# Hybrid DiT layer on one core: norm columns turned by TensorE before they are stored, and another order of the seven products and of their weight sums

## The chip, the cores and the metric

The kernel runs on one core of a Trainium2 chip. The metric is device time in microseconds (us) of one execution; the time before is the median of three executions. A separate execution was recorded by the hardware profiler, and all rows below are of that one. PE is TensorE (its weight loads, PEld, overlap it), DVE is VectorE, ACT is ScalarE, POOL is GpSimd and SP is SyncE; POOL and SP here do little but issue transfers.

## The reference, cut to what matters

One layer for 512 tokens of width 1024: a token mixer (retention, 2-D Fourier mixing, spatial gating) between two modulated norms, then an MLP with squared ReLU between two more. All data are float32.

```python
mod = silu(c) @ w_mod + b_mod
sh1, sc1, gt1, sh2, sc2, gt2 = split(mod, 6)
h = modulate(rms_norm(x, g_pre_mix), sh1, sc1)
y = token_mixer(h, ...)          # sum over branches: sigmoid gate * (branch @ w), then @ w_out
x = x + gt1 * rms_norm(y, g_post_mix)
h2 = modulate(rms_norm(x, g_pre_mlp), sh2, sc2)
x = x + gt2 * rms_norm(relu(h2 @ w_up) ** 2 @ w_down, g_post_mlp)   # hidden width 4096
```

## The kernel before

**Precision.** A float32 product is made of three matmuls: every operand is split into a high part (written by ACT: `whi`, `rhi`, `phi`) and a low part (raw minus high part, by DVE: `wlo`, `rlo`, `plo`), and high x high, high x low and low x high are summed in PSUM (L132 to L134, L1025, L1152). Weights arrive as 512 KB chunks, 128 x 1024, on SP's queue.

**Stages in time.** Modulation and norms; the projections with retention, Fourier and gating; the gates (to about 340 us), the branch products ("abc" loop, eight turns of `m`), the output projection `out_proj` (to about 440 us); then the MLP in four quarters of the hidden width. For quarters q = 0, 1, 2 the down product is `down(q)`; then `up(q + 1, m)` makes the next quarter's hidden units in eight turns of 24 matmuls. The last quarter's down product is plain (`last_down`).

**The seven products.** `down(q)` is one level of Strassen's scheme: seven products (`seventh`, L1141) of 24 matmuls each. Their weights are quarters of `w_down` or sums of these: L11, S1 = L21 + L22, L12, S3 = L11 + L21, S2 = S1 + L11, L22, S4 = S2 + L12, each in two halves a = 0, 1. Their other operands are hidden units: `r1`, `r2` (R11, R21, R22) or sums of them: `t13` (T1, T3), `t24` (T2, T4), made on DVE with `sums_13` and `sums_24` and split by ACT and DVE. The products stand in three pairs of PSUM banks, `chain`, `side` and `own`; after most products `collect` (L1155) adds the pair into `y2`, on DVE except in quarter 0, where those that set `y2` go to ACT. A later product that continues the same pair has to wait for the `collect` that reads it.

**Weight sums.** `weights_to(q, upto)` makes weights in the order of the table `order` (L1029). `rawL` gets L11 (SP) and then, by a DVE add (L1059), L21, so it holds S3. `rawS` is loaded with L21 (L1057) and grows by accumulating transfers: L22 at L1060 (S1), L11 at L1069 (S2), L12 at L1072 (S4). Accumulating transfers are issued by POOL, each after the split of the sum before.

**What sets the order.** PE, SP and POOL keep the order of the program text, whose calls put weights some products ahead. ACT and DVE are ordered by a list scheduler at build time, in which splits and collects have a raised priority. All engines work in order: what stands behind a waiting instruction waits too.

**Modulation rows.** `background()` loads one 512 KB chunk of `w_mod` (POOL, L388) and does one product of it with c as a DVE instruction of 1.28 us (L241), giving a column of 128 values of `mod`. The calls are spread over the gates, the abc loop, and, for the last group (gt2), over the up loop of quarter 1.

**The norm columns.** `gg1` = gt1 * g_post_mix and `gg2` = gt2 * g_post_mlp come out as 128 x 8 columns (value p + 128 k at partition p, column k). `spread_row` (L848) turns such a column into a row that is the same on all partitions: L851 writes it into DRAM in row order, 1024 pieces of 4 bytes, and L853 loads that back to 128 partitions. `gg1r` is used by `out_proj` (z, L907), `gg2r` by `last_down`. Both transfers are on POOL's queue. `ident`, the unit matrix used for transposes on PE (L929), is loaded by SP.

Of the kernel before, what the change touches and what calls it, by code (L numbers as in the profile page):

```python
# [35 lines left out]
def kernel(ctx: ExitStack, tc: tile.TileContext, i: dict, out: bass.AP):  # L36
# [764 lines left out]
    for n in range(12, 24):  # L801
        gate(n)
        background()

    gg1 = const.tile([P, KT], F32, name="gg1")
    gs2 = const.tile([P, KT], F32, name="gs2")
# [7 lines left out]
    merged = []  # L814
    for m in range(KT):
        w = chunk("abc", m)
        pss = [bank() for _ in range(3)]
        for k in (4, 5, 6, 7, 0, 1, 2, 3):
            b = 0 if k < 4 else (1 if k < 6 else 2)
            sl = slice(128 * k, 128 * k + 128)  # L820
            mm3(pss[b], (w[0][:, sl], w[1][:, sl]), hl(branch_in[k]), k in (0, 4, 6), k in (3, 5, 7))
        acc = []
        for b in (1, 2, 0):
            n = 8 * b + m
            t = tmp(f"mg{b}")
# [21 lines left out]

    def spread_row(col, name):  # L848

        d = dram.tile([D], F32, name=name + "_d")  # L850
        nc.gpsimd.dma_start(out=d.rearrange("(k p) -> p k", p=P), in_=col)  # L851
        r = slot([P, D], F32, name)
        nc.gpsimd.dma_start(out=r, in_=d.unsqueeze(0).broadcast_to([P, D]))  # L853
        return r
# [3 lines left out]
    for t in range(TT):  # L858
        nc.sync.dma_start(out=xts[t], in_=i["x"][t])
    pad = slot([P, D], F32, "pad")  # L860
    ident, used = pad[:, 0:P], [P]
    nc.sync.dma_start(out=ident, in_=i["eye"])
    gg1_row = spread_row(gg1, "gg1r")
    h2 = [slot([P, 2, L], F32R, "h2") for _ in range(KT)]
# [105 lines left out]
    def sums_13(a0, a1, b1):  # L970
# [6 lines left out]
        return ta[:, E0]  # L977

    def sums_24(t1, b1, b0):

# [47 lines left out]

    order = [(x, a) for x in ("L11", "S1", "L12", "S3", "S2", "L22", "S4") for a in range(2)]  # L1029
    ws_ = {}  # L1030
# [3 lines left out]
    def weights_to(q, upto):  # L1034

        while made.setdefault(q, 0) < min(upto, len(order)):
            x, a = order[made[q]]
# [15 lines left out]
            if x == "L11":  # L1053
                rawL[a] = slot([P, D], F32, "rawL")
                nc.sync.dma_start(out=rawL[a], in_=l11)
                rawS[a] = slot([P, D], F32, "rawS") if q else raw_pool.tile([P, D], F32, name="rawS", tag="wmod2", bufs=2)
                nc.gpsimd.dma_start(out=rawS[a], in_=l21)  # L1057
                parts(pair(), rawL[a])
                V.tensor_tensor(out=rawL[a], in0=rawL[a], in1=rawS[a], op=ALU.add)  # L1059
                nc.gpsimd.dma_start(out=rawS[a], in_=l22, accum_op=ALU.add)  # L1060
            elif x in ("L12", "L22"):
# [3 lines left out]
            elif x == "S3":  # L1065
                parts(pair(), rawL[a])
            elif x == "S1":
                parts(pair(slot), rawS[a], 0)
                nc.gpsimd.dma_start(out=rawS[a], in_=l11, accum_op=ALU.add)  # L1069
            elif x == "S2":  # L1070
                parts(pair(), rawS[a])
                nc.gpsimd.dma_start(out=rawS[a], in_=l12, accum_op=ALU.add)  # L1072
            else:
                parts(pair(), rawS[a])

    early, tas = [], []

    def up_first_done(half):
# [14 lines left out]
        if half:  # L1093
            weights_to(0, 8)
            for k in range(4):
                sums_24(tas[k], late[1][:, k], early[1][:, k])
            for k in range(4):
                split(r2[k][:, 0, E1], r2[k][:, 1, E1], late[1][:, k])

# [37 lines left out]
    def down(q, following):  # L1137
# [3 lines left out]
        def seventh(pss, w, x, first, ahead):  # L1141
            for a in range(2):
                weights_to(q, ahead + a)
                if ahead + a > len(order):
                    following(ahead + a - len(order))
                wa = ws_.pop((w, a))
# [18 lines left out]
        collect(chain, 0, 0, False, True)  # L1165
        seventh(own, "L12", "R21", True, 7)
        collect(own, 0, 0, False)
        seventh(side, "S3", "T3", True, 9)
        collect(side, 1, 1, True, True)
        seventh(chain, "S2", "T2", False, 11)  # L1170
        collect(chain, 0, 1, True, True)
        seventh(side, "L22", "T4", False, 13)
        collect(side, 0, 1, True)
        seventh(chain, "S1", "T1", False, 15)
        collect(chain, 1, 1, True)
        seventh(chain, "S4", "R22", False, 16)
# [6 lines left out]
    for q in range(3):  # L1183
# [3 lines left out]
        for n, m in enumerate(turns if q < 2 else range(KT)):  # L1187
            up(q + 1, m, 7 - n if q < 2 else 2)
            if q == 0:
                background()  # L1190
            if q < 2 and n >= 4:
                weights_to(q + 1, n - 3)
        if q == 0:
            V.tensor_tensor(out=gg2, in0=mod[:, 5], in1=vecs[:, G_POST2], op=ALU.mult)
    gg2_row = spread_row(gg2, "gg2r")
    xts[:] = [slot([P, D], F32, "xt") for _ in range(TT)]
# [133 lines left out]
```

## Time and profile before

| what | us |
|---|---|
| median of three executions | 785.85 (784.85, 787.02, 785.85) |
| the profiled execution: its own time | 782.69 |
| its span, first to last instruction | 780.2 |
| PE busy | 761.8 (98%) |
| DVE busy | 547.4 (70%) |
| ACT busy | 398.0 (51%) |
| POOL busy | 61.0 (8%) |

The span is what the rows can account for; around it lie 2.5 us of start and end. The profiled execution was 3.2 us below the median of the three. In the rows a time in front is counted from the start of the span, the next figure is the duration, and square brackets hold the idle time of that engine before the instruction and what ended it. "a<-b" names what is written and read.

### The profile page before, as it was taken

How to read it: one execution, taken by the hardware profiler on the slowest of the kernel's cores; microseconds unless marked ns; L12 is line 12 of the kernel's file. 1: busy time of each engine (PE TensorE's matmuls, PEld its weight loads, DVE VectorE, ACT ScalarE, POOL GpSimd, SP SyncE). 2: the span in 40 equal slices, each digit the busy share in tenths (PEclk: the TensorE clock that was granted, in tenths of full speed). 3: DMA queues.
4: the chain of work that ended last, by engine and by line, in shares of the span. 5: the costliest groups of instructions: out<-in, count | busy, mean ns of one | idle time of the engine just before them, and what ended most of it. 6: DMA issues, size and time to landing. Idle time of an engine off the chain costs nothing.

```text
span 780.2 us, 9628 instructions
## 1 busy us (share of the span) xinstructions
PE 761.8 (98%) x3628; PEld 636.3 (82%) x3628; DVE 547.4 (70%) x853; ACT 398.0 (51%) x599; POOL 61.0 (8%) x107
## 2 busy tenths in 40 slices
PE   9999999999999999999999999899997999999996
PEld 6888888888888878888888998688876887888885
DVE  6999997777889546589748648637974468634544
ACT  6337557658887534233246457436632466236411
POOL 1061000000000101101000000001210001100000
PEclk9999999999999999999999999999999999999999
DMA  9954242643333458667423634447855526834211
GB/s 349 383 186 136 95 134 67 206 152 104 113 108 100 143 181 276 218 194 269 145 98 109 217 55 108 108 155 242 196 99 176 173 61 168 260 117 136 81 55 54
DMA packets 34461, 121.44 MB, mean 156 GB/s; under 512 B 4184, under 2 KB 4448, under 8 KB 34416
## 3 DMA queue, kind: packets, MB, share of 16 engines
q1 hardware_dynamic: 24768, 86.17, 32.3%
q0 software_dynamic: 9632, 34.66, 16.7%
q8 instruction: 28, 0.46, 0.3%
q14 instruction: 17, 0.14, 0.1%
q10 hardware_dynamic: 16, 0.01, 0.0%
HBM read 116.62 MB, written 4.20 MB: 155 GB/s over the span
## 4 chain that ended last, share of the span: by engine, by line
PE 66%; issue 19%; DVE 7%; DMA 5%; ACT 2%; POOL 1%; DVEq 0%; POOLq 0%; ACTq 0%
PE ps L134 15%; PE ps L133 15%; PE ps L132 14%; PE pu L1025 6%; PE kq L357 5%; PE chain L1152 4%; DMA rawS<-in_w_down 4%; PE side L1152 2%; DMA wmod<-in_w_modT 2%; DVE wlo L128 1%; PE warm L190 1%; DVE y L1162 1%; POOL wmod L388 1%; DVE t L128 1%; DVE wlo L109 1%
## 5 line engine op out<-in xcount | busy, mean ns | idle before, releaser
L134 PE MATMUL ps<-h,wlo 128*128 128x512 f32 x448 | 174.8, 390 | 1.9 <-DVE wlo L109 1.9
L132 PE MATMUL ps<-h,whi 128*128 128x512 f32 x448 | 175.1, 391 | 0.0
L133 PE MATMUL ps<-h,whi 128*128 128x512 f32 x448 | 174.6, 390 | 0.0
L106 ACT ACTIVATE whi<-raw 128x1024 fp32r<-128x1024 f32 (+1 forms) x97 | 100.8, 1041 | 138.0 <-PE ps L133 86.5
L109 DVE TENSOR_TENSOR wlo<-raw,whi 128x1024 fp32r<-128x1024 f32 (+1 forms) x97 | 116.4, 1200 | 71.9 <-ACT whi L106 71.7
L134 PEld LDWEIGHTS ps<-h,wlo 128*128 128x128 f32 x448 | 84.1, 188 | 20.2 <-DVE wlo L109 2.7
L132 PEld LDWEIGHTS ps<-h,whi 128*128 128x128 f32 x448 | 84.1, 188 | 17.7 <-ACT whi L106 0.4
L133 PEld LDWEIGHTS ps<-h,whi 128*128 128x128 f32 x448 | 84.2, 188 | 17.3
L241 DVE CUSTOM_DVE_ANT_0 wmod<-wmod,cb,vecs 128x1024 f32<-128x1024 f32 x32 | 41.0, 1281 | 28.2 <-DMA wmod<-in_w_modT 28.2
L388 POOL DMA_DIRECT2D wmod<-in_w_modT x32 | 17.1, 535 | 328.8 <-PE ps L134 253.8
L1025 PE MATMUL pu<-h,rhi 128*128 128x256 f32 x224 | 39.9, 284 | 0.2 <-DVE pad L881 0.2
L1152 PE MATMUL chain<-whi,r 128*128 128x512 f32 x96 | 31.9, 404 | 4.0 <-DVE y L1162 4.0
L1025 PEld LDWEIGHTS pu<-h,rhi 128*128 128x128 f32 x224 | 34.4, 192 | 0.5 <-DVE pad L881 0.4
L1152 PE MATMUL side<-whi,t 128*128 128x512 f32 x96 | 30.6, 390 | 0.0
L1025 PE MATMUL pu<-h,rlo 128*128 128x256 f32 x112 | 29.8, 283 | 0.0
L106 ACT ACTIVATE rhi<-raw 128x1024 fp32r<-128x1024 f32 x17 | 17.8, 1056 | 22.6 <-DMA raw<-in_w_out 16.3
L128 DVE TENSOR_TENSOR wlo<-rawS,whi 128x1024 fp32r<-128x1024 f32 x12 | 14.6, 1225 | 18.0 <-ACT whi L127 18.0
L357 PE MATMUL kq<-h,whi 128*128 128x512 f32 x112 | 27.0, 392 | 0.0
L127 ACT ACTIVATE whi<-rawS 128x1024 fp32r<-128x1024 f32 x12 | 12.7, 1060 | 27.9 <-DMA rawS<-in_w_down 18.7
L1152 PEld LDWEIGHTS chain<-whi,r 128*128 128x128 f32 x96 | 18.7, 195 | 8.4 <-issue 4.4
L357 PEld LDWEIGHTS kq<-h,whi 128*128 128x128 f32 x112 | 21.0, 188 | 4.8 <-ACT h L253 0.4
L109 DVE TENSOR_TENSOR rlo<-raw,rhi 128x1024 fp32r<-128x1024 f32 x17 | 20.6, 1222 | 5.5 <-ACT rhi L106 5.5
(359 smaller groups left out, 1641.3 us busy)
## 6 DMA issues: line engine op xcount, KB each, us to landing
wmod<-in_w_modT POOLq DMA_DIRECT2D x32, 512.0 KB, 3.6
raw<-in_w_up SPq DMA_DIRECT2D x32, 512.0 KB, 3.5
raw<-in_w_gate SPq DMA_DIRECT2D x24, 512.0 KB, 3.9
rawS<-in_w_down POOLq DMA_DIRECT2D x24, 512.0 KB, 5.4
raw<-in_w_down SPq DMA_DIRECT2D x20, 512.0 KB, 4.6
wmod<-in_w_modT SPq DMA_DIRECT2D x16, 512.0 KB, 8.6
raw<-in_w_kq SPq DMA_DIRECT2D x8, 512.0 KB, 7.1
raw<-in_w_v SPq DMA_DIRECT2D x8, 512.0 KB, 4.2
```

The costliest lines, as they stand in the source:

```text
L106: S.activation(out=hi, in_=raw, func=AF.Copy)
L109: rest = lambda: V.tensor_tensor(out=lo, in0=raw, in1=f32(hi), op=ALU.subtract)
L127: S.activation(out=dst_hi, in_=src, func=AF.Copy)
L128: V.tensor_tensor(out=dst_lo, in0=src, in1=f32(dst_hi), op=ALU.subtract)
L132: PE.matmul(ps, w[0], x[0], start=first, stop=False)
L133: PE.matmul(ps, w[0], x[1], start=False, stop=False)
L134: latest[0] = PE.matmul(ps, w[1], x[0], start=False, stop=last)
L241: return V.tensor_tensor_reduce(out=prod, in0=wt, in1=cvec, scale=1.0, scalar=bias_col, op0=ALU.mult, op1=ALU.add, accum_out=dst_col)
L357: PE.matmul(kq[n], w[sub % 2][:, 128 * n:128 * n + 128], hs[k][:, sub // 2], start=k == 0 and sub == 0, stop=False)
L388: load = nc.gpsimd.dma_start(out=t, in_=i["w_modT"][j, k])
L1025: latest[0] = PE.matmul(ps, w[a][:, 128 * m:128 * m + 128], x[b], start=k == 0 and (a, b) == parts[0] and m % 2 == 0, stop=k == KT - 1 and ...
L1152: latest[0] = PE.matmul(pss[p], st[b], mv[c], start=first and a == 0 and kk == 0 and n == 0, stop=a == 1 and kk == 1 and n == 2, skip_grou ...
```

## The change

1. **Norm columns.** `to_dram` turns the column by a PE transpose into an 8 x 128 tile of PSUM, ACT copies it into `pad`, and one transfer of eight 512-byte pieces writes it to DRAM. For `gg1` this stands in the abc loop at m = 2, for `gg2` in the last up loop at n = 5. The unit matrix is loaded earlier, by POOL instead of SP.
2. **Weight sums.** L21 gets into `rawL` by an accumulating transfer (L1086 of the changed kernel) instead of the DVE add. The load of `rawS` with L21 and the accumulation of L22 stand back to back on POOL, at S1's place.
3. **Quarter 0.** `sums_24` is cut in two: the first halves before the products (`sums_2`), the second halves (`second_24`), which only the sixth product's operand T4 needs, after S3's collect; the splits of R22 come after S2's collect.
4. **Quarters 1 and 2.** The weights are made in the order S1, L11, S3, S2, L12, L22, S4, begun at the first turn of the up loop instead of the fifth; the products run L11, S3, S2, L12, S1, L22, S4.
5. **The last modulation rows** are loaded and multiplied in the up loop of the last quarter, two a turn, instead of that of quarter 1.

```diff
+    def to_dram(col, name):
+        ps = bank("psv")
+        PE.transpose(ps[0:KT, 0:P], col, ident)
+        row = pad[0:KT, (4 if name == "gg1" else 5) * P:][:, 0:P]
+        S.copy(out=row, in_=ps[0:KT, 0:P])
+        d = dram.tile([KT, P], F32, name=name + "_d")
+        nc.gpsimd.dma_start(out=d, in_=row)
+        return d
...
     for m in range(KT):
+        if m == 2:
+            gg1_d = to_dram(gg1, "gg1")
...
-        d = dram.tile([D], F32, name=name + "_d")
-        nc.gpsimd.dma_start(out=d.rearrange("(k p) -> p k", p=P), in_=col)
         r = slot([P, D], F32, name)
-        nc.gpsimd.dma_start(out=r, in_=d.unsqueeze(0).broadcast_to([P, D]))
+        nc.gpsimd.dma_start(out=r, in_=d.rearrange("k p -> (k p)").unsqueeze(0).broadcast_to([P, D]))
...
+    def sums_2(t1, b1):
+        tb = tmp("tb")
+        V.scalar_tensor_tensor(out=tb[:, E0], in0=t1, scalar=-1.0, in1=b1, op0=ALU.mult, op1=ALU.subtract)
+        t24.append(aux([P, 2, L], F32R, "t24"))
+        split(t24[-1][:, 0, E0], t24[-1][:, 1, E0], tb[:, E0])
+        tbs.append(tb)
+    def second_24(k):
+        tb = tbs[k]
+        V.scalar_tensor_tensor(out=tb[:, E1], in0=tb[:, E0], scalar=-1.0, in1=early[1][:, k], op0=ALU.mult, op1=ALU.subtract)
+        split(t24[k][:, 0, E1], t24[k][:, 1, E1], tb[:, E1])
...
             if x == "L11":
                 rawL[a] = slot([P, D], F32, "rawL")
                 nc.sync.dma_start(out=rawL[a], in_=l11)
-                rawS[a] = slot([P, D], F32, "rawS") if q else raw_pool.tile([P, D], F32, name="rawS", tag="wmod2", bufs=2)
-                nc.gpsimd.dma_start(out=rawS[a], in_=l21)
                 parts(pair(), rawL[a])
-                V.tensor_tensor(out=rawL[a], in0=rawL[a], in1=rawS[a], op=ALU.add)
-                nc.gpsimd.dma_start(out=rawS[a], in_=l22, accum_op=ALU.add)
+                nc.gpsimd.dma_start(out=rawL[a], in_=l21, accum_op=ALU.add)
...
             elif x == "S1":
-                parts(pair(slot), rawS[a], 0)
+                rawS[a] = slot([P, D], F32, "rawS") if q else raw_pool.tile([P, D], F32, name="rawS", tag="wmod2", bufs=2)
+                nc.gpsimd.dma_start(out=rawS[a], in_=l21)
+                nc.gpsimd.dma_start(out=rawS[a], in_=l22, accum_op=ALU.add)
+                parts(pair(slot), rawS[a])
                 nc.gpsimd.dma_start(out=rawS[a], in_=l11, accum_op=ALU.add)
...
+        else:
+            seventh(side, "S3", "T3", True, 7)
+            collect(side, 1, 1, True, True)
+            seventh(chain, "S2", "T2", False, 9)
+            collect(chain, 0, 1, True, True)
+            seventh(own, "L12", "R21", True, 11)
+            collect(own, 0, 0, False)
+            seventh(chain, "S1", "T1", False, 13)
+            collect(chain, 1, 1, True)
+            seventh(side, "L22", "T4", False, 15)
+            collect(side, 0, 1, True)
         seventh(chain, "S4", "R22", False, 16)
         collect(chain, 1, 0, False, True)
...
-            if q == 0:
-                background()
-            if q < 2 and n >= 4:
-                weights_to(q + 1, n - 3)
-        if q == 0:
-            V.tensor_tensor(out=gg2, in0=mod[:, 5], in1=vecs[:, G_POST2], op=ALU.mult)
-    gg2_row = spread_row(gg2, "gg2r")
+            if q < 2:
+                weights_to(q + 1, (1, 2, 2, 2, 3, 4, 4, 4)[n])
+            if q == 2 and n < 4:
+                background(2)
+            if q == 2 and n == 5:
+                V.tensor_tensor(out=gg2, in0=mod[:, 5], in1=vecs[:, G_POST2], op=ALU.mult)
+                gg2_d = to_dram(gg2, "gg2")
+    gg2_row = spread_row(gg2_d, "gg2r")
```

DVE in quarter 0, from the low part of S3's second half to that of S2 (`wlo<-rawS`), before the change. `t_..<-tb` are low parts of `t24`, `r_..<-late` those of R22.

```order
L128 TENSOR_TENSOR wlo<-rawL,whi 128x1024
L1162 TENSOR_TENSOR y_4336<-y_4336,own 128x512
L128 TENSOR_TENSOR t_4292<-ta,t_4292 128x512
L128 TENSOR_TENSOR t_4306<-tb,t_4306 128x512
L983 SCALAR_TENSOR_TENSOR tb<-tb,early 128x256
L982 SCALAR_TENSOR_TENSOR tb<-ta,late 128x256 x2
L983 SCALAR_TENSOR_TENSOR tb<-tb,early 128x256 x2
...
L128 TENSOR_TENSOR t_4324<-tb,t_4324 128x512
L128 TENSOR_TENSOR r_3980<-late,r_3980 128x256
L128 TENSOR_TENSOR wlo<-rawS,whi 128x1024 x2
```

The same place of the changed kernel.

```order
L128 TENSOR_TENSOR wlo<-rawL,whi 128x1024
L1190 TENSOR_TENSOR y_4327<-y_4327,own 128x512
L128 TENSOR_TENSOR t_4295<-ta,t_4295 128x512
L128 TENSOR_TENSOR t_4308<-tb,t_4308 128x256
L128 TENSOR_TENSOR t_4313<-tb,t_4313 128x256
L995 SCALAR_TENSOR_TENSOR tb<-ta,late 128x256
L128 TENSOR_TENSOR wlo<-rawS,whi 128x1024
L128 TENSOR_TENSOR t_4318<-tb,t_4318 128x256
L995 SCALAR_TENSOR_TENSOR tb<-ta,late 128x256
L128 TENSOR_TENSOR wlo<-rawS,whi 128x1024
```

The first low part of S2 has moved ahead of most sums and splits of `t24` and ahead of all those of R22 that stood in front of it.

DVE in quarter 1 before, from the collect of S3 (`side`) to that of S4 (the last `chain`); `wlo<-raw` at L128 is the low part of L22, and the `wlo<-rawS` rows are those of S4.

```order
L1162 TENSOR_TENSOR y_4338<-y_4338,side 128x512
L128 TENSOR_TENSOR wlo<-raw,whi 128x1024 x2
L1162 TENSOR_TENSOR y_4335<-y_4335,chain 128x512
L1162 TENSOR_TENSOR y_4336<-y_4336,chain 128x512
L128 TENSOR_TENSOR wlo<-rawS,whi 128x1024 x2
L1162 TENSOR_TENSOR y_4335<-y_4335,side 128x512
L1162 TENSOR_TENSOR y_4336<-y_4336,side 128x512
L109 TENSOR_TENSOR wlo<-raw,whi 128x1024
L1162 TENSOR_TENSOR y_4337<-y_4337,chain 128x512
L1162 TENSOR_TENSOR y_4338<-y_4338,chain 128x512
```

The changed kernel from the collect of L12 (`own`) on.

```order
L1190 TENSOR_TENSOR y_4327<-y_4327,own 128x512
L128 TENSOR_TENSOR wlo<-rawS,whi 128x1024
L1190 TENSOR_TENSOR y_4328<-y_4328,chain 128x512
L1190 TENSOR_TENSOR y_4329<-y_4329,chain 128x512
L128 TENSOR_TENSOR wlo<-rawS,whi 128x1024
L1190 TENSOR_TENSOR y_4326<-y_4326,side 128x512
L1190 TENSOR_TENSOR y_4327<-y_4327,side 128x512
L109 TENSOR_TENSOR wlo<-raw,whi 128x1024 x2
L1190 TENSOR_TENSOR y_4328<-y_4328,chain 128x512
L1190 TENSOR_TENSOR y_4329<-y_4329,chain 128x512
```

S1's collect (the first pair of `y_4328` and `y_4329`) now stands ahead of the second low part of S4, and L22's product lies between S1's and S4's.

POOL's transfers around the end of the abc loop, before.

```order
L388 DMA wmod2_3113<-in_w_modT 128x1024
L1057 DMA rawS_4093<-in_w_down 128x1024
L1057 DMA rawS_4127<-in_w_down 128x1024
L853 DMA gg1r_3305<-gg1r_d_3303 128x1024
L922 DMA kept0_3402<-xt_3293 128x1024
```

The changed kernel there.

```order
L816 DMA gg1_d_3027<-pad_2923 8x128
L388 DMA wmod2_3073<-in_w_modT 128x1024
L388 DMA wmod2_3120<-in_w_modT 128x1024
L1095 DMA rawS_4156<-in_w_down 128x1024
L1096 DMA rawS_4156<-in_w_down 128x1024
L1095 DMA rawS_4188<-in_w_down 128x1024
L1096 DMA rawS_4188<-in_w_down 128x1024
L867 DMA gg1r_3308<-gg1_d_3027 128x1024
L933 DMA kept0_3405<-xt_3300 128x1024
```

The load of `gg1r` now has two accumulating transfers (L1096) in front of it, each of which waits until the load of the same `rawS` has landed.

## Rows read from the trace of the kernel before

**Rows 1.** The page, busy time of the engines in the whole span.

```profile
PE 761.8 (98%) x3628; PEld 636.3 (82%) x3628; DVE 547.4 (70%) x853; ACT 398.0 (51%) x599; POOL 61.0 (8%) x107
```

**Rows 2.** Waits of PE: engine, line, waited for; us in total, times, longest.

```profile
PE chain L1152 <- DVE y L1162: 4.0, 1, 4.0
PE chain L1152 <- DVE wlo L128: 2.6, 1, 2.6
PE ps L134 <- DVE wlo L109: 1.9, 2, 1.5
...
PE side L1152 <- DVE wlo L128: 1.1, 1, 1.1
PE own L1152 <- DVE wlo L128: 0.5, 1, 0.5
```

**Rows 3.** Stretches: length, then busy us of PE, PEld, DVE, ACT, POOL, clock, DMA.

```profile
493.00:498.00 5.00, 5.00 (x22) 4.16 (x23) 3.25 (x3) 1.66 (x2) 1.70 (x2) 1.00 0.64 107
596.36:599.00 2.64, 2.64 (x8) 2.07 (x9) 0.46 (x1) 0.00 (x0) 0.00 (x0) 0.62 0.61 199
...
700.00:740.00 40.00, 40.00 (x178) 33.16 (x177) 19.03 (x20) 22.22 (x31) 0.00 (x0) 1.00 0.37 119
```

**Rows 4.** Gate stage, 264 to 289 us: timelines of POOL and DVE, and transfers (KB, landing).

```profile
268.57 0.92 POOL L851 DMA_DIRECT2D gg1r_d<-gg  x1 [4.83 <-DVE gg L808]
269.49 0.55 POOL L388 DMA_DIRECT2D wmod<-in_w_modT  x1
...
281.76 1.28 DVE L241 CUSTOM_DVE_ANT_0 wmod<-wmod,cb,vecs 128x1024 f32<-128x1024 f32 x1 [9.32 <-DMA wmod<-in_w_modT]
...
gg1r_d<-gg POOLq DMA_DIRECT2D x1, 4.0 KB, 11.0
...
wmod<-in_w_modT POOLq DMA_DIRECT2D x32, 512.0 KB, 3.6
```

**Rows 5.** Timeline of DVE in quarter 0, around S2's weights.

```profile
486.59 0.69 DVE L128 TENSOR_TENSOR t<-tb,t 128x512 fp32r<-128x512 f32 x1
...
491.68 2.36 DVE L128 TENSOR_TENSOR wlo<-rawS,whi 128x1024 fp32r<-128x1024 f32 x2
```

**Rows 6.** Quarter 1, 566 to 604 us: timelines of POOL, ACT, DVE and PE.

```profile
572.32 0.93 POOL L851 DMA_DIRECT2D gg2r_d<-gg  x1 [0.79 <-DVE gg L1194]
...
587.30 1.06 ACT L127 ACTIVATE whi<-rawS 128x1024 fp32r<-128x1024 f32 x1 [7.49 <-DMA rawS<-in_w_down]
...
592.07 1.23 DVE L128 TENSOR_TENSOR wlo<-rawS,whi 128x1024 fp32r<-128x1024 f32 x1 [2.44 <-ACT whi L127]
...
596.36 0.47 PE L1152 MATMUL chain<-whi,r 128*128 128x512 f32 x1 [3.97 <-DVE y L1162]
...
603.51 0.39 PE L132 MATMUL ps<-h,whi 128*128 128x512 f32 x1
```

**Rows 7.** Line L1072 (L12 into `rawS`), then all `rawS` transfers: KB, us to landing.

```profile
DMA to landing us min/median/max: 5.1/8.0/12.6
...
rawS<-in_w_down POOLq DMA_DIRECT2D x24, 512.0 KB, 5.4
```

**Rows 8.** End of the abc loop: POOL, DVE; landing of `rawS` loads (L1057), of `gg1r`.

```profile
362.26 0.53 POOL L1057 DMA_DIRECT2D rawS<-in_w_down  x1 [3.45 <-DVE mod L241]
...
370.10 0.53 POOL L1057 DMA_DIRECT2D rawS<-in_w_down  x1 [7.30 <-DVE mod L241]
370.62 0.53 POOL L853 DMA_DIRECT2D gg1r<-gg1r_d  x1
...
386.00 0.69 DVE L907 TENSOR_TENSOR z<-ps,gg1r 128x512 f32<-128x512 f32 x1 [2.21 <-ACT junk L875]
...
DMA to landing us min/median/max: 4.8/6.5/8.1
...
DMA to landing us min/median/max: 7.0/7.0/7.0
```

**Rows 9.** Transposes on PE (L929): duration ns min/median/max, first and last start.

```profile
L929 PE MATMUL psT<-pad,z x32: 271/273/274, 400.4 to 441.8; 128*128 128x128 f32 x32
```

More of the change, by code (lines that the diff above doesn't have):

```diff
@@ L803 @@
         background()
+    pad = slot([P, D], F32, "pad")
+    ident, used = pad[:, 0:P], [P]
+    nc.gpsimd.dma_start(out=ident, in_=i["eye"])
+    def to_dram(col, name):
[6 more added lines that the diff above has]
+        return d
     gg1 = const.tile([P, KT], F32, name="gg1")
@@ L846, with spread_row @@
     fhs = [slice(0, 512), slice(512, 1024)]
-    def spread_row(col, name):
-        d = dram.tile([D], F32, name=name + "_d")
-        nc.gpsimd.dma_start(out=d.rearrange("(k p) -> p k", p=P), in_=col)
+    def spread_row(d, name):
         r = slot([P, D], F32, name)
-        nc.gpsimd.dma_start(out=r, in_=d.unsqueeze(0).broadcast_to([P, D]))
+        nc.gpsimd.dma_start(out=r, in_=d.rearrange("k p -> (k p)").unsqueeze(0).broadcast_to([P, D]))
         return r
@@ L859 @@
         nc.sync.dma_start(out=xts[t], in_=i["x"][t])
[L860 to L863, printed above, removed]
+    gg1_row = spread_row(gg1_d, "gg1r")
     h2 = [slot([P, 2, L], F32R, "h2") for _ in range(KT)]
@@ L977, in sums_13 @@
         return ta[:, E0]
+    tbs = []
+    def sums_2(t1, b1):
[8 more added lines that the diff above has]
+        split(t24[k][:, 0, E1], t24[k][:, 1, E1], tb[:, E1])
     def sums_24(t1, b1, b0):
@@ L1027, in up_first @@
                                   stop=k == KT - 1 and (a, b) == parts[2], skip_group_check=True)
-    order = [(x, a) for x in ("L11", "S1", "L12", "S3", "S2", "L22", "S4") for a in range(2)]
+    orders = [[(x, a) for x in o for a in range(2)] for o in (("L11", "S1", "L12", "S3", "S2", "L22", "S4"),
+                                                              ("S1", "L11", "S3", "S2", "L12", "L22", "S4"))]
     ws_ = {}
@@ L1034, in weights_to @@
     def weights_to(q, upto):
+        order = orders[q > 0]
         while made.setdefault(q, 0) < min(upto, len(order)):
@@ L1074, in weights_to @@
                 parts(pair(), rawS[a])
-    early, tas = [], []
+    early, lates, tas = [], [], []
     def up_first_done(half):
@@ L1094, in up_first_done @@
             weights_to(0, 8)
+            lates.extend(late)
             for k in range(4):
-                sums_24(tas[k], late[1][:, k], early[1][:, k])
-            for k in range(4):
-                split(r2[k][:, 0, E1], r2[k][:, 1, E1], late[1][:, k])
+                sums_2(tas[k], late[1][:, k])
     zs = {}
@@ L1143, in seventh @@
                 weights_to(q, ahead + a)
-                if ahead + a > len(order):
-                    following(ahead + a - len(order))
+                if ahead + a > len(orders[0]):
+                    following(ahead + a - len(orders[0]))
                 wa = ws_.pop((w, a))
@@ L1165, in down @@
         collect(chain, 0, 0, False, True)
[L1166 to L1175, printed above, removed]
+        if q == 0:
+            seventh(own, "L12", "R21", True, 7)
+            collect(own, 0, 0, False)
+            seventh(side, "S3", "T3", True, 9)
+            collect(side, 1, 1, True, True)
+            for k in range(4):
+                second_24(k)
+            seventh(chain, "S2", "T2", False, 11)
+            collect(chain, 0, 1, True, True)
+            for k in range(4):
+                split(r2[k][:, 0, E1], r2[k][:, 1, E1], lates[1][:, k])
+            seventh(side, "L22", "T4", False, 13)
+            collect(side, 0, 1, True)
+            seventh(chain, "S1", "T1", False, 15)
+            collect(chain, 1, 1, True)
+        else:
+            seventh(side, "S3", "T3", True, 7)
+            collect(side, 1, 1, True, True)
+            seventh(chain, "S2", "T2", False, 9)
+            collect(chain, 0, 1, True, True)
+            seventh(own, "L12", "R21", True, 11)
+            collect(own, 0, 0, False)
+            seventh(chain, "S1", "T1", False, 13)
+            collect(chain, 1, 1, True)
+            seventh(side, "L22", "T4", False, 15)
+            collect(side, 0, 1, True)
         seventh(chain, "S4", "R22", False, 16)
```

## The prediction

> **What bounds the kernel now.** I read the busy times of the page first: PE works 761.8 of 780.2 us [rows 1]. PE is the bound, the change takes no product away, and so it can win only in the 18.4 us in which PE stands still, and in stretches where its clock is down. The waits of PE come next, since they name those places: five kinds add up to 10.1 us [rows 2]. 4.0 is `chain` in quarter 1, at S4; 2.6 is `chain` in quarter 0, at S2; 1.1 is `side` at S3 of quarter 1; 0.5 is `own` in quarter 2; and of the 1.9 at L134 the one wait of 1.5 lies in the gate stage, the rest in the output projection. What is left of the 18.4 is the start and the tail behind the last product, which the change does not touch. For each place I then went to the timelines of the engine waited for and of whatever that engine waited for.
>
> *Gate stage.* POOL issues the write of the `gg1` column at 268.57 and behind it, at 269.49, a 512 KB chunk of modulation rows. The column takes 11.0 us for 4 KB; the chunk lands at 281.76, 12.3 us after its issue, where the median for this kind is 3.6 [rows 4]. DVE has idled 9.32 us for it, its later work is late, and PE waits 1.5. The place of the late landing, right behind the column, is my ground for calling the column the cause.
>
> *Quarter 1, S4.* The same thing: the `gg2` column is issued at 572.32, and the accumulation of L12 into `rawS` behind it needs 12.6 us instead of 5.4 [rows 6, 7]. ACT idles 7.49 until 587.30, the second low part of S4 comes only at 592.07 on DVE, the collect of S1, which has lower place in DVE's order, follows, and S4, which continues S1's banks, starts at 596.36 after 3.97 of idle. Then the clock is down: 0.62 of full speed in the next 2.6 us [rows 3], between the two levels of 1.2 and 2.4 GHz, so part of the stretch ran at the lower one. S4's 24 matmuls take 603.51 − 596.36 = 7.15 us [rows 6]; at the pace of 22 in 5.00 us, measured just after the 2.6 us wait of quarter 0 at full clock [rows 3], they take 5.45. So this wait costs 3.97 + 1.70 = 5.67, and the shorter one of quarter 0 lost no clock.
>
> *Quarter 0, S2.* DVE works without a gap from 486.59 to 491.68, on `t24` and R22, before the first low part of S2 [rows 5]. It is saturated there, and no transfer is involved.
>
> **The change part by part.**
>
> *Columns.* With the eight 512-byte pieces instead of 1024 pieces of 4 bytes I take the queue as free again after the usual time. The trace has no transfer of this shape on POOL; bounds are the 3.6 of a chunk of 512 KB in longer runs and 11.0 as now. I take the former, since its pieces are nearer to the chunk's [rows 4]. Gain in the gate stage: 1.5. Both columns move as well, so that at 11.0 the stall would follow the `gg1` write into the abc loop, and the `gg2` write into the last quarter, where DVE is busy 19 of 40 us and PE never waits [rows 3]. Price: two transposes of 0.27 [rows 9] at most, on the path, less 0.1 for overlap: 0.4; the ACT copies are far shorter than ACT's idle time.
>
> A rule of the Trainium skill speaks against this step. DMA: Bandwidth & Descriptors, section Anatomy of one DMA, fits one POOL transfer as 2.0 us and its bytes over 436 GB/s, whatever its pieces; by it the 4 KB column would take 2 us, block nobody, and the step would give nothing: the sum below would be smaller by 1.5. Its section Rules for kernel authors says on the other hand that a strided last dimension becomes one descriptor per element. The measured 11.0 us [rows 4] sides with the second.
>
> *Quarter 0.* In front of the first low part of S2, between the two rows of [rows 5], stood 5.1 us of work. By the order, two half splits and one half sum stay of it, with a full split running 0.6 apart and half pieces about 0.34: 1.0 us. So this low part starts some 4.1 us earlier, which is more than the 2.6 that PE waited. 1.5 us are to spare; the second one has a further split and sum in front, 0.7, and is needed half a product, 2.7 us, later. What was moved is late next: T4's second halves and R22's splits. They are needed one and two products on (5.45 us each), with some 4 us of work among them. Nothing left: gain 2.6.
>
> *Quarters 1 and 2.* S1's weights are made first, during the up loop, where DVE is also rid of the last modulation rows (seven times 1.28 us). The S3 wait of 1.1 and the L12 wait of 0.5 were of low parts that came behind too much other work; with the earlier start and without the DVE adds they go. S1 and S4 are now a product apart, so that S1's collect has 5.45 us before S4 needs the banks, and the sum S4 is asked for a product after S1 still, but without a column in the way: gain 3.97 + 1.70. The new order's own demand is S3's second half: the accumulation of L21 into `rawL` can be issued only after the low part of L11's second half, which I place 3.1 us before the quarter's first product, from the order and the durations of 1.06 for a high and 1.23 for a low part [rows 6]. At 5.4 [rows 7] it lands 2.3 after that product's start; the high part and the low part, behind other work, are done at 6.3, and are needed 1.5 products in, at 8.2. 1.9 us to spare. Bounds: nothing, up to the 12.6 of the slowest landing, which would cost between 3.6 and 5.3 (below).
>
> *POOL's queue.* `gg1r` is now behind two accumulations. The load issued at 362.26 took the longer 8.1, to 370.4; then 0.9 for issuing the accumulation (the column's issue took 0.93 [rows 6]), the second load at 371.3 with 4.8, to 376.1, another 0.9, and `gg1r` at 377.0 instead of 370.62. With its 7.0 it lands at 384.0; z wants it at 386.0 [rows 8]. 2 us to spare; with 8.1 for the second load too it lands at 387.3, 1.3 late, and if `gg1r` took a column's neighbour's time on top, at some 390. What stands behind z on DVE is the low part of the next output weights, for which PE has the short wait in [rows 2], so lateness would cost PE its full length. I take 0.3, between nothing and 3.9. The `gg2` write comes after six turns of the last up loop, 6 × 5.45 = 33 us from its start, and the row is wanted after eight turns and a first down product, 49 us; a write of 3.6 and a load of 7.0 end at 44, so nothing. With 11.0 for each it would be 6 late.
>
> *Sum.* 1.5 + 2.6 + 1.1 + 3.97 + 1.70 + 0.5 = 11.4; less 0.4 and 0.3: 10.7. The span goes from 780.2 to 769.5, the profiled execution from 782.69 to 772.0. The median of three is 3.2 above the profiled execution; taking the difference as it is, 785.85 − 10.7 = **775.1**.
>
> **Rivals.**
> - *One wait stays.* Either S2 of quarter 0 still finds DVE late (2.6 stay: 777.7), or `gg1r` is late (up to 3.9, and if PE stands that long the clock falls as at S4, 1.7: 779 to 780.7), or the gate chunk is late for a reason other than the column (1.5: 776.6). For it: each has only 1 to 2 us to spare, in an order fixed at build time. Against: the margins rest on measured durations.
> - *The new order starves S3.* The accumulations into `rawL` land as slowly as the slowest L12 did, 12.6 [rows 7], in quarters 1 and 2. For it: SP's loads of weights and POOL's accumulations fall together there, and a sum that DVE made in a moment now takes a transfer. Then PE waits about 4.5 at S3 and loses 1.7 of clock, twice: 12.4 in place of the 10.7 won, 787.5, slower. It decides from landings of about 12 us on. Against: the 12.6 stood behind a column, and the median is 5.4. In one quarter alone it would give 781.3.
> - *The change doesn't do what it says.* If small pieces weren't the cause and landings of 12 us come from the load on the queues, 1.5 stays in the gate and S4 may still be late by what its new slack, a product, doesn't cover: 776.6 to 779.
>
> **How the numbers follow.** All waits go: 0.62, 773 to 777 with the spread of the three medians (1.2 up, 1.0 down). One stays, or the third rival: 0.26, 776 to 781. S3 starved once: 0.04, near 781; twice or worse: 0.08 with all else that I can't see, half of it within the bound and half above. A measurement of this kernel tells about 0.3%, 2.4 us, from no change. Faster: 0.62 + 0.26 + 0.04 = 0.92, of which I give 0.02 to "same" for waits that add up; same 0.06, slower 0.04. The range 772.5 to 780.5 leaves out the starved cases and the tail of the second.
>
> **What would show it.** In the profile after: `chain` at L1152 (its new line) without waits over 0.5 us; the `gg1` write landing in under 4 us and no modulation chunk over 8; `gg1r` landed before z asks for it; clock 1.00 through S4 of quarter 1; PE idle near 8 us. It is wrong if a wait of `side` on the low part of `rawL` appears in quarters 1 or 2, or one of z on `gg1r`.

## The result, and the profile after

The changed kernel takes 775.13 us (median of four executions, 774.15 to 776.58); the kernel before takes 785.55 on the same chip (784.85 to 787.02). The ratio is 0.9866, with a 95% interval of 0.984 to 0.989: faster by 1.1 to 1.6%. The forecast was 775.1. The profiled execution took 774.27 with a span of 771.9, against 782.69 and 780.2: 8.3 us less, where the medians differ by 10.4 and the forecast of the span was 10.7 less. Both profiled executions are at the low end of their kernel's times, and that of before lies below all four behind its median. So the time came out as forecast, but not its parts.

The page of the changed kernel, busy times of the engines:

```profile
PE 759.5 (98%) x3630; PEld 634.9 (82%) x3630; DVE 541.9 (70%) x851; ACT 398.9 (52%) x605; POOL 66.2 (9%) x114
```

Its waits of PE (engine, line, waited for; total, times, longest), which answer to [rows 2]:

```profile
PE ps L133 <- DVE wlo L109: 3.0, 3, 1.6
PE warm L190 <- POOL eps_h L168: 1.0, 1, 1.0
PE ssx L274 <- DVE sq L272: 0.5, 2, 0.3
PE ps L134 <- DVE wlo L109: 0.3, 1, 0.3
PE pu L1052 <- DVE pad L892: 0.2, 1, 0.2
```

All waits of `chain`, `side` and `own` are gone, and the 1.5 in the gate stage too; the 0.3 at L134 was there before. New are three waits at L133, 3.0 us together, and 0.5 at the start (`ssx`), which comes and goes from run to run. Where they lie is seen from when PE gets to each stage. First some operations by line or tile in the kernel before (count, duration in ns, first and last start), then the same in the changed one: the branch products, the first up product, the `chain` products on R11 and R22, and the last down product.

```profile
L132 PE MATMUL ps<-sguT,whi x16: 388/389/390, 337.4 to 376.2; 128*128 128x512 f32 x16
L1025 PE MATMUL pu<-h,rhi x224: 277/284/386, 426.2 to 470.6; 128*128 128x256 f32 x112
L1152 PE MATMUL chain<-whi,r x96: 387/390/629, 473.6 to 685.7; 128*128 128x512 f32 x96
L132 PE MATMUL ps<-whi,a x24: 389/390/390, 736.2 to 772.3; 128*128 128x512 f32 x24
```

```profile
L132 PE MATMUL ps<-sguT,whi x16: 389/389/398, 335.5 to 374.4; 128*128 128x512 f32 x16
L1052 PE MATMUL pu<-h,rhi x224: 277/283/386, 426.0 to 470.4; 128*128 128x256 f32 x112
L1180 PE MATMUL chain<-whi,r x96: 389/389/396, 473.4 to 674.8; 128*128 128x512 f32 x96
L132 PE MATMUL ps<-whi,a x24: 389/389/397, 725.5 to 763.9; 128*128 128x512 f32 x24
```

At the branch products the changed kernel is 1.9 us ahead (337.4 to 335.5); at the first up product only 0.2, so 1.7 were lost in the output projection; at the last S4 product it is 10.9 ahead, so quarters 0 to 2 gave 10.7; at the last matmul only 8.4, so 2.5 were lost in the last quarter.

*The loss in the output projection* is the late `gg1r`. Timelines of POOL, DVE and PE, and the landing of the `rawS` loads (L1095), to set beside [rows 8]:

```profile
360.71 0.53 POOL L1095 DMA_DIRECT2D rawS<-in_w_down  x1 [3.64 <-DVE mod L241]
369.19 0.91 POOL L1096 DMA_DIRECT2D rawS<-in_w_down  x1 [7.95 <-DMA rawS<-in_w_down]
369.75 0.90 POOL L1095 DMA_DIRECT2D rawS<-in_w_down  x1
379.39 0.88 POOL L1096 DMA_DIRECT2D rawS<-in_w_down  x1 [8.74 <-DMA rawS<-in_w_down]
379.94 0.86 POOL L867 DMA_DIRECT2D gg1r<-gg_d  x1
...
386.14 0.69 DVE L918 TENSOR_TENSOR z<-ps,gg1r 128x512 f32<-128x512 f32 x1 [4.28 <-ACT rhi L106]
...
388.02 0.50 PE L133 MATMUL ps<-wlo,merged 128*128 128x512 f32 x1 [1.63 <-DVE wlo L109]
...
DMA to landing us min/median/max: 4.0/7.8/9.1
```

POOL waits 7.95 and 8.74 us for the two `rawS` loads before it may issue the accumulations, and only then `gg1r`, which lands 6.1 us after its issue at 379.94, at 386.0. z, which could have started some 1.9 us sooner, starts at 386.14, and the low part behind z makes PE stand for 1.63. The row of z names ACT as the releaser, whose work ended at 386.1 too; e5 below, where z starts at 384.2, shows that it was `gg1r`.

*The loss in the last quarter* lies behind the `gg2` row. Timelines of POOL, ACT and PE:

```profile
714.16 0.55 POOL L867 DMA_DIRECT2D gg2r<-gg_d  x1 [4.79 <-DMA gg_d<-pad]
714.70 2.09 POOL L1243 DMA_DIRECT2D xt<-kept  x4
...
724.19 1.06 ACT L106 ACTIVATE whi<-raw 128x1024 fp32r<-128x1024 f32 x1 [2.60 <-DMA raw<-in_w_down]
...
726.56 0.50 PE L133 MATMUL ps<-wlo,a 128*128 128x512 f32 x1 [0.70 <-DVE wlo L109]
...
728.93 0.50 PE L133 MATMUL ps<-wlo,a 128*128 128x512 f32 x1 [0.71 <-DVE wlo L109]
```

The row and four reloads of x, 2.5 MB, are issued within 3 us, while SP fetches the last `w_down` chunks; in the kernel before they were issued between 664.8 and 679.0, ahead of the last quarter. ACT waits 2.60 for a chunk, and PE twice.

The section on the kernel before is wrong in one sentence: POOL does not keep the order of the text. In the text the load of `gg1r` stands ahead of the `rawS` loads, and POOL issues it behind them, in the kernel before as in the changed one. The order shown for the change holds.

### The profile page after: what moved, and what is told of

Its sections match the earlier page's. It is cut to its first block, busy times and chain, and to the rows that moved or that the text cites. A ratio compares the mean times of both kernels' runs of the same rounds, so it can differ in the third digit from the quotient of the medians.

```text
span 771.9 us, 9640 instructions
## 1 busy us (share of the span) xinstructions
PE 759.5 (98%) x3630; PEld 634.9 (82%) x3630; DVE 541.9 (70%) x851; ACT 398.9 (52%) x605; POOL 66.2 (9%) x114
## 4 chain that ended last, share of the span: by engine, by line
PE 93%; DVE 3%; DMA 2%; ACT 1%; issue 1%; SPq 0%; DVEq 0%; ACTq 0%
PE ps L134 21%; PE ps L133 21%; PE ps L132 21%; PE chain L1180 8%; PE pu L1052 6%; PE kq L357 5%; PE side L1180 4%; PE own L1180 2%; DMA x<-in_xT 1%; DMA raw<-in_w_down 1%; DVE wlo L109 1%; PE ps L474 0%; PE ps L473 0%; PE ps L472 0%; DVE rlo L109 0%
## 5 line engine op out<-in xcount | busy, mean ns | idle before, releaser
L134 PE MATMUL ps<-h,wlo 128*128 128x512 f32 x448 | 174.5, 390 | 0.3 <-DVE wlo L109 0.3
L133 PE MATMUL ps<-h,whi 128*128 128x512 f32 x448 | 174.4, 389 | 0.0
L134 PEld LDWEIGHTS ps<-h,wlo 128*128 128x128 f32 x448 | 84.1, 188 | 18.7 <-DVE wlo L109 1.3
L133 PEld LDWEIGHTS ps<-h,whi 128*128 128x128 f32 x448 | 84.1, 188 | 17.4
L388 POOL DMA_DIRECT2D wmod<-in_w_modT x32 | 17.1, 534 | 327.3 <-PE ps L134 275.1
L1180 PEld LDWEIGHTS side<-whi,t 128*128 128x128 f32 x96 | 18.0, 188 | 3.7
```

Source lines behind the costliest of these rows:

```text
L133: PE.matmul(ps, w[0], x[1], start=False, stop=False)
L134: latest[0] = PE.matmul(ps, w[1], x[0], start=False, stop=last)
L388: load = nc.gpsimd.dma_start(out=t, in_=i["w_modT"][j, k])
L1180: latest[0] = PE.matmul(pss[p], st[b], mv[c], start=first and a == 0 and kk == 0 and n == 0, stop=a == 1 and kk == 1 and n == 2, skip_grou ...
```

## The experiments

Ratios are to the kernel before on the same chip. e1 to e4 shared one chip, e5 to e7 another, e8 to e11 a third, and e12 ran on a fourth.

**e1: the rows alone**, put into the kernel before.

```diff
     for m in range(KT):
+        if m == 2:
+            gg1_d = to_dram(gg1, "gg1")
...
         if q == 0:
             V.tensor_tensor(out=gg2, in0=mod[:, 5], in1=vecs[:, G_POST2], op=ALU.mult)
+            gg2_d = to_dram(gg2, "gg2")
```

> The kernel before, with nothing but the norm columns turned on PE and stored as rows (gg1 in the abc loop, gg2 still before quarter 1's seven products). Theory, the 4-byte column write blocks the transfers behind and beside it: the 1.5 us gate wait and the 4.0 us wait at S4 of quarter 1 with its 1.7 us of lower clock go, the waits at S2 of quarter 0 (2.6) and S3 of quarter 1 (1.1) stay; 785.5 - 7.2 + 0.4 = 778.7 us. Rival, the long landing comes from the load on the queues and S4 needs the new order: at most 1.5 us are won, about 784.4 us, and the wait of chain on y stays.

Measured: 782.78 us, 0.996 (0.995 to 0.998). The waits of PE:

```profile
PE psv L812 <- DVE gg L1205: 6.0, 1, 6.0
PE chain L1163 <- DVE wlo L128: 2.6, 1, 2.6
```

The waits at the gate and at S4 are gone, as the theory has it; that at S3 is gone too, which the theory left in place. But the time of 778.7 was missed by 4, for a reason that neither side had: a transpose on PE makes PE wait for the value. `gg2` is ready only when DVE has done the last modulation row and what stands in front of it there. PE stood 6.0 us for it, and the granted clock behind it was 0.69, between its two levels of 1.2 and 2.4 GHz (stretches as in [rows 3], the first behind the wait of 2.6):

```profile
492.00:496.00 4.00, 4.00 (x13) 3.17 (x13) 1.42 (x2) 0.34 (x1) 1.42 (x2) 0.67 0.72 117
566.00:572.00 6.00, 6.00 (x20) 4.76 (x19) 2.51 (x5) 1.69 (x2) 0.56 (x1) 0.69 0.69 153
```

With the column it was POOL that waited for the value, not PE. The moved modulation rows are thus what makes the turned `gg2` affordable, not a by-work. The 6.0 us also gave DVE and the transfers time ahead of quarter 1's products, so e1 alone does not tell whether S3 and S4 lost their waits with the column or through this delay; e8 and e12 do.

**e2: the old order of weights and products**, with the new weight sums.

```diff
-        order = orders[q > 0]
+        order = orders[0]
...
-        if q == 0:
+        if True:
             seventh(own, "L12", "R21", True, 7)
...
-            if q < 2:
-                weights_to(q + 1, (1, 2, 2, 2, 3, 4, 4, 4)[n])
+            if q < 2 and n >= 4:
+                weights_to(q + 1, n - 3)
```

> The changed kernel with the old order of weights and products in quarters 1 and 2 (also begun at the fifth turn of the up loop again); rows, quarter 0 and modulation rows as changed. Theory, the S4 wait came from the column write: no wait of chain on y, only 1.1 at S3 and 0.5 at L12 come back; 775.1 + 1.6 = 776.7 us. Rival, it was the order: the wait at S4 and the clock loss return, 775.1 + 1.6 + 5.7 = 782.4 us.

Measured: 795.57, 1.013 (1.011 to 1.016), slower than the kernel before and outside of both forecasts. POOL and PE in quarter 1:

```profile
558.02 0.89 POOL L1095 DMA_DIRECT2D rawS<-in_w_down  x1
565.83 0.86 POOL L1096 DMA_DIRECT2D rawS<-in_w_down  x1 [6.93 <-DMA rawS<-in_w_down]
574.16 0.87 POOL L1098 DMA_DIRECT2D rawS<-in_w_down  x1 [7.46 <-DVE plo L128]
...
580.72 0.50 PE L1180 MATMUL chain<-whi,t 128*128 128x512 f32 x1 [1.29 <-ACT whi L127]
```

A sum in `rawS` is a chain of a load and two accumulations, each started after the one before has landed: from 558.0 to about 579.6 for S2's second half. With the load moved to S1's place and begun late, PE waits for S2 four times in each of two quarters, 11.9 us in all, and works at a lower clock behind these waits (0.64 to 0.79 from 576 to 588 us). So the new weight sums need the new order or its earlier start, which this run does not separate. What the order would be worth without the new sums it does not tell either; e8 leaves out both.

**e3: the columns back**, in the changed kernel.

```diff
-        PE.transpose(ps[0:KT, 0:P], col, ident)
...
-        nc.gpsimd.dma_start(out=d, in_=row)
+        nc.gpsimd.dma_start(out=d.rearrange("k p -> p k"), in_=col)
```

> The changed kernel with both columns written as before, 1024 pieces of 4 bytes (gg1 in the gate stage, gg2 in the last up loop), all else as changed. Theory: the gate wait of 1.5 returns, the gg2 write lands after about 11 us instead of 4.8 and holds up w_down chunks on SP, so the last quarter gets 0 to 4 us worse: 776.6 to 780.6 us. Rival, small pieces do not matter: 775.1 us, modulation chunks behind the column land in under 5 us.

Measured: 786.03, 1.0015 (0.9995 to 1.0035): without the rows the whole gain is gone. The PE waits and the transfers of the last quarter (700 to 740 us: KB, landing):

```profile
PE ps L132 <- ACT a L127: 8.1, 1, 8.1
PE ps L134 <- DVE wlo L109: 1.9, 2, 1.6
...
gg_d<-gg POOLq DMA_DIRECT2D x1, 4.0 KB, 10.7
raw<-in_w_down SPq DMA_DIRECT2D x7, 512.0 KB, 9.1
...
GB/s 401 389 160 365 53 266 287 229 238 82 164 20 45 37 33 25 8 12 70 254 381 414 307 381 406 426 422 410 414 410 397 123 25 0 0 0 0 0 0 0
```

The last line is what all queues moved in each us from 700 on. The gate wait is back, and the `gg2` column, issued at 707.4 where `w_down` chunks are fetched, takes 10.7 us and pushes their landing to 9.1: PE waits 8.1 and works at a lower clock afterwards. The theory had the mechanism, its price, 1.5 to 5.5, was at most about half of the 10.9 measured (786.03 against 775.13, on another chip). By the two profiles 8.5 us were lost in the last quarter and 3.9 at the gate, where the clock fell behind the wait of 1.6 (0.57 from 288 to 292 us); the output projection got 1.5 back, since PE came there later and its wait for the late `gg1r` shrank to 0.3.

**e4: quarter 0's sums whole again.**

```diff
-                sums_2(tas[k], late[1][:, k])
+                sums_24(tas[k], late[1][:, k], early[1][:, k])
+            for k in range(4):
+                split(r2[k][:, 0, E1], r2[k][:, 1, E1], late[1][:, k])
```

> The changed kernel with quarter 0's sums and splits whole and in front of the products again; all else as changed. Theory: DVE is late for S2 again, a wait of about 2.6 us of chain on the low part from rawS, 777.7 us. Rival, the accumulating transfer in place of the DVE add and the lighter queue already suffice: under 0.5 us of wait, 775.1 us.

Measured: 779.38, 0.991 (0.989 to 0.994), 4 us more than the changed kernel. The wait is the old one:

```profile
PE chain L1182 <- DVE wlo L128: 2.6, 1, 2.6
```

The profiled execution took 775.55 at a mean clock of 0.998; the five timed ones took 778.3 to 780.5 at 0.993 to 0.996. In e1 the same wait of 2.6 was followed by a clock of 0.67 in the next 4 us, here in the profile it was not. So I estimate the wait at 2.6 or, with the 1.7 of clock seen at S4, about 4.3, by execution. The profiled execution was also spared the wait for `gg1r`: the second `rawS` load was there 7.9 us after its issue instead of 9.6, and PE got to the first up product at 424.4 instead of 426.0.

**e5, e6, e7: the two new waits.** e5 moves the load of the `gg1` row to SP's queue, e6 the reloads of x ahead of the last up loop, e7 does both.

```diff
-        nc.gpsimd.dma_start(out=r, in_=d.rearrange("k p -> (k p)").unsqueeze(0).broadcast_to([P, D]))
+        (nc.sync if name == "gg1r" else nc.gpsimd).dma_start(out=r, in_=d.rearrange("k p -> (k p)").unsqueeze(0).broadcast_to([P, D]))
...
+        if q == 2:
+            xts[:] = [slot([P, D], F32, "xt") for _ in range(TT)]
+            for t in range(TT):
+                nc.gpsimd.dma_start(out=xts[t], in_=kept[t])
         for n, m in enumerate(turns if q < 2 else range(KT)):
```

> The changed kernel with the load of the gg1 row on SP's queue, behind the four x loads, instead of POOL's behind the two accumulations into rawS. Theory, the load is late because it stands behind them: it lands some 10 us earlier, the wait of 1.6 us in the output projection falls to 0.3, 775.1 - 1.3 = 773.8 us. Rival, the transfer engines are full there and the load only displaces output weights behind it on SP: 775.1 us or slower, with a wait on another weight.

> The changed kernel with the four reloads of x (2 MB) issued on POOL ahead of the last up loop instead of behind the gg2 row. Theory, the reloads and the gg2 row take bandwidth from the w_down chunks on SP at the start of the last down product: the two waits of 0.7 us at its low parts go, 775.1 - 2.0 = 773.1 us. Rival, the w_down chunks are late by themselves (buffers come free late): waits stay, 775.1 us.

> Both: gg1 row on SP and reloads of x ahead of the last up loop. If the two waits are independent, 775.1 - 1.3 - 2.0 = 771.8 us; if one of the moves only shifts a wait, 773 to 774 us.

Measured: e5 772.67, 0.984 (0.982 to 0.986); e6 773.27, 0.985 (0.983 to 0.987); e7 772.11, 0.983 (0.981 to 0.986). In e5 the wait in the output projection is gone, and z starts at 384.2; in e6 the two waits for low parts of `w_down` are gone, and one of 0.6 for a low part of the hidden units has come. In e7's profile, which is of the slowest of its six executions, a new one of 1.5 appears, of PE for the last hidden units:

```profile
PE ps L132 <- ACT a L127: 1.5, 1, 1.5
...
719.87 1.06 ACT L106 ACTIVATE whi<-raw 128x1024 fp32r<-128x1024 f32 x1 [3.32 <-DMA raw<-in_w_down]
720.84 0.58 ACT L968 ACTIVATE relu<-ps 128x512 f32<-128x512 f32 x1
...
722.93 0.61 ACT L127 ACTIVATE a<-relu 128x512 fp32r<-128x512 f32 x1
```

The scheduler, with the reloads elsewhere, has put a high part of `w_down` in front of the last ReLU on ACT, and that high part waits 3.32 us for its chunk. In e6 the order is the same and the wait of ACT 2.69; the 0.6 of PE comes from it. Each gain against the changed kernel's 0.987 lies within what the intervals leave open.

**e8: without the new weight sums and without the new order.**

```diff
             if x == "L11":
-                nc.gpsimd.dma_start(out=rawL[a], in_=l21, accum_op=ALU.add)
+                V.tensor_tensor(out=rawL[a], in0=rawL[a], in1=rawS[a], op=ALU.add)
+                nc.gpsimd.dma_start(out=rawS[a], in_=l22, accum_op=ALU.add)
...
-        order = orders[q > 0]
+        order = orders[0]
```

> The changed kernel without its new weight sums and its new order in quarters 1 and 2 (DVE add into rawL, rawS loaded at L11's place, old products): rows, quarter 0's split sums and the moved modulation rows stay. Theory, the column write alone made the S4 and S3 waits: no wait of chain on y, at most 0.5 to 1.6 us of waits in quarters 1 and 2, so 775 to 777 us. Rival, the order is needed for S4: 4.0 and 1.7 come back, about 781 us.

**e9: the changed kernel again**, beside it.

> The changed kernel again, as the reference for the runs beside it on this chip: 775.1 us, within 1.5.

Measured: e8 773.69, 0.9855 (0.983 to 0.988); e9 775.18, 0.9876 (0.985 to 0.990). The waits of PE in e8 in the MLP:

```profile
PE ps L133 <- DVE wlo L109: 1.5, 2, 0.8
...
PE own L1180 <- DVE wlo L128: 0.8, 2, 0.5
```

No wait at S3 or S4: towards these the new sums and the new order give nothing that the other three parts don't. They save the 0.8 of `own` and cost the wait for `gg1r`, which e8 hasn't got, since no accumulation stands in front of that load. By time e8 and e9 can't be told apart: their intervals overlap. In e9 that wait was 1.84, and in this execution the clock fell behind it. Stretches around it (length, busy us by engine, clock):

```profile
388.00:392.00 4.00, 3.67 (x10) 2.90 (x11) 1.41 (x2) 0.34 (x1) 0.00 (x0) 0.61 0.66 206
392.00:396.00 4.00, 4.00 (x19) 3.23 (x18) 2.29 (x7) 2.00 (x5) 0.00 (x0) 0.96 0.14 56
```

**e10, e11: other places for the last quarter's loads**, in the changed kernel with the `gg1` row on SP; the reloads of x on POOL are taken out.

```diff
                     wd[4 * fh + a] = chunk("down", 24 + 4 * fh + a)
+                if fh:
+                    for u in range(TT):
+                        nc.sync.dma_start(out=xts[u], in_=kept[u])
...
-            if q == 2 and n < 4:
-                background(2)
-            if q == 2 and n == 5:
+            if q == 2 and n < 3:
+                background(3)
+            if q == 2 and n == 4:
```

The second piece is in e11 alone.

> The changed kernel with the gg1 row on SP and the reloads of x on SP's queue too, behind the last w_down chunk. If the two waits of 0.7 us in the last down product come from the reloads, they go and nothing new comes, since x is wanted only some 10 us later: 775.1 - 1.3 - 2.0 = 771.8 us. If the gg2 row alone already delays the chunks: one of them stays, 773 us.

> As the one before, and the last modulation rows three a turn with gg2 made and turned one turn (5.45 us) earlier. If gg2's row then lands before the last w_down chunks are wanted, no wait is left in the last quarter: 771.5 us. If PE now waits for gg2, as at the transpose of the rows-only kernel: over 774 us.

Measured: both 774.56, 0.986 (0.983 to 0.9885); e10 missed both of its figures, e11 came out by its second. Each traded its wait for another: in e10 PE waits 2.7 for the last hidden units, as in e7; in e11, as in e1, for `gg2` itself:

```profile
PE ps L132 <- ACT a L127: 2.7, 1, 2.7
...
703.49 0.38 PE L812 MATMUL psv<-pad,gg 128*8 128x128 f32 x1 [2.86 <-DVE gg L1238]
```

**e12: e8 with the modulation rows one quarter earlier.**

```diff
-            if q == 2 and n < 4:
-                background(2)
-            if q == 2 and n == 5:
+            if q == 1:
+                background()
+            if q == 2 and n == 1:
```

> The kernel of e8 (without the new weight sums and order) with the last modulation rows in the up loop ahead of quarter 2, one a turn, and gg2 turned on PE in the second turn of the last up loop: the gg2 row and the reloads of x are then out of the way when the last w_down chunks come. If these loads are what makes the waits at the start of the last down product: no wait there, span 772.2 - 2.0 = 770.2 us, about 772 us, 0.983 of before. If DVE gets too late for quarter 2's sums with seven products of 1.28 us more: waits of chain or side on low parts there, no gain.

Measured: 772.00, 0.984 (0.981 to 0.986), span 770.1. No wait is left in the last quarter. One of 1.3 at `side`, at S3 of quarter 2, which has the seven modulation products in front of it now, and one of 0.3 at `own` in quarter 1 are left (the last line is the landing of L12 into `rawS`, L1101):

```profile
PE side L1180 <- DVE wlo L128: 1.3, 1, 1.3
...
PE own L1180 <- DVE wlo L128: 0.3, 1, 0.3
...
DMA to landing us min/median/max: 5.3/5.6/5.9
```

Quarter 2 of e12 repeats quarter 1 of the kernel before without the column: it has the old order, the old sums, and the same modulation products on DVE ahead of it. S3 waits there as it did, and S4 does not.

All its six times (771.5 to 773.6) lie below all nine of the changed kernel (774.15 to 777.2), though on different chips, and the intervals of the ratios overlap. By time it can't be told from e5 to e8 either; I would build on it, since it has the least PE waits and three of the five parts of the change.

## Why the prediction came out

*What bounds the kernel.* Right: PE's waits were the gain, and the places named are empty now. One reading was wrong: the short wait at L134, 0.3, which the prediction puts in the output projection, lies between 100 and 200 us in both kernels and does not stand behind z.

*Columns.* Right in mechanism, and larger than its term. Landing of the 8 x 128 writes (L816) and of the modulation chunks (L388) in the changed kernel:

```profile
DMA to landing us min/median/max: 3.2/4.0/4.8
...
DMA to landing us min/median/max: 3.4/3.6/6.3
```

The slowest chunk needs 6.3 instead of 12.2, and the changed kernel is 1.9 ahead behind the gate for the forecast 1.5. Every column here lands after 10.3 to 11.0 us, and e3 shows the price, 10.9 us at its places. The fit in the Trainium skill (DMA: Bandwidth & Descriptors, Anatomy of one DMA) has no term for the number of pieces and gives 2.0 us for 4 KB; for the columns it does not hold, and the measurement decides.

*Quarter 0.* Right, 2.6, and sometimes the clock on top (e4).

*Quarters 1 and 2.* Right in size; the causes were credited in part to the wrong parts of the change. S4's wait came from the column, as read: in quarter 2 of e12 L12 lands after 5.9 at most instead of 12.6, and S4 does not wait, though the order is the old one. S3's wait did not come from the column. In the kernel before, the low part that PE waits for there was already running when the column was issued, at 572.32 [rows 6]; DVE had been busy without a gap for the 11 us before it:

```profile
571.93 1.22 DVE L128 TENSOR_TENSOR wlo<-rawL,whi 128x1024 fp32r<-128x1024 f32 x1
...
573.21 0.50 PE L1152 MATMUL side<-wlo,t 128*128 128x512 f32 x1 [1.07 <-DVE wlo L128]
```

So it was "too much other work", as I had it, but what took the work away is the move of the seven modulation products: the wait is gone in e8, which has the old start and the DVE adds, and back in e12, where the products stand ahead of quarter 2. I gave it to the earlier start and the missing adds, and counted the order as part of what frees S4. The order and the sums are worth 0.8 of waits and cost 1.6. The three quarters gave 10.7 for 9.9; a part of the 0.8 is the slower first matmul behind each wait (0.47 instead of 0.39 us at S4), which the idle times leave out, and the rest is not traced.

*POOL's queue.* The step that failed: I took 0.3 from a second `rawS` load of 4.8; it landed after 9.1, POOL issued what stands behind it 9.6 us after it, and the wait was 1.63. The 2 us to spare rested on that one figure: in e4's profile the same load was there after 7.9, and PE did not wait. This is the rival "one wait stays", with `gg1r`, and one of the prediction's own signs of being wrong, z waiting on `gg1r`.

*The last quarter.* "So nothing" was wrong by 2.5, of which the transpose, 0.2, was allowed for. I had asked whether `gg2r` comes in time, and it does; I had not asked what it and the reloads of x behind it do to the `w_down` chunks on SP. With the reloads moved (e6) the two waits for chunks go, so they were the cause of these. But of the 2.5 only 1.1 comes back: from the last S4 product to the last matmul e6 takes 88.0 us, the changed kernel 89.1 and the kernel before 86.6. In e6 PE waits behind the new order on ACT instead, where a high part waits 2.69 for a `w_down` chunk that is still late. In e12, with the same order on ACT, it is 86.7; there the `gg2` row comes some 23 us earlier and the seven loads of modulation chunks have left the last quarter. Which of these two makes the chunk late in e6 no run separates.

*The total* fits by chance within its last 2 us. In the span the gate gave 0.4 and the three quarters 0.8 more than forecast; the output projection lost 1.7 for 0.5 (0.3 and a transpose), the last quarter 2.5 for 0.2, and the tail 0.1. That leaves the span 2.4 above the forecast (771.9 for 769.5). The other way went the distance of the median from the profiled execution, which I had taken as fixed: 3.2 before, 0.9 after (775.13 and 774.27). Most of this distance is the clock. Of 54 executions of the kernel before on the four chips of e1 to e12, the 7 with a mean granted clock of 0.996 or more took 782.1 to 783.8 us, and the 18 with 0.990 or less took 785.2 to 787.8; the profiled one had 0.996. The changed kernel's nine had 0.995 to 0.998. So an execution of the kernel before usually loses more by its clock than the one I read, and it seems that a part of that went with the waits. The starved S3 did not come: the slowest accumulation into `rawL` landed after 9.7, and no PE wait followed.

## What to carry to other kernels

A small strided store can be the slowest thing in its neighbourhood: look at what lands late right behind it, on all queues, before reordering the work that waits. Turning the data on PE is cheap here (0.27 us), but it puts PE behind the data's producer, so place it where that producer is long done. When a transfer is moved, ask what else wants the transfer engines then, not only whether it lands in time; and undo the parts of a change one by one: here two of five brought no gain that a run shows, and one that looked like a by-work, the move of the modulation products, freed S3. A run that takes a cause away may shift the engines against each other as well (e1), so look for a run in which everything else stays.

## What the runs showed of the hardware

- While a 4 KB column of 4-byte pieces is on its way, the transfers of all queues all but stop: in e3 from 711 to 718 us they moved 8 to 45 GB/s together, against 307 to 426 in the ten us from 720 on; in the kernel before 1 to 41 from 269 to 280 us and 33 to 49 from 575 to 584. The same 4 KB as eight rows land in 1.6 to 4.8 us over all runs.
- An accumulating transfer of 512 KB lands in some 5.5 us (5.0 to 10.1 in the changed kernel); a sum of three is over 20 us long with its waits (e2).
- The granted clock fell after waits of PE of 1.56 (e3, gate), 1.84 (e9) and 2.6 us (e1), to 0.57, 0.61 and 0.67 in the next 4 us, and stayed at 1.00 after waits of 1.53 (the kernel before, gate), 1.63 (the changed kernel), 1.94 (e6) and 2.63 (e4's profile). So waits of the same length cost some 1.7 us more in some executions: in the 9.66 us behind it e9 started 35 matmuls, the changed kernel 43. What decides is not shown.
